# Up projection of a hybrid encoder: three row pairs by seven products in five groups of eleven, and the gate rows in two lots

## The chip, the cores and the metric

The kernel runs on one core of a Trainium2 chip. The metric is the device time of one execution in microseconds (us). Engines are named as the profile names them: PE is TensorE (matrix products), PEld its weight loads, DVE is VectorE, ACT is ScalarE, POOL is GpSimd and SP is SyncE, which only issues transfers here.

## The reference

Two layers of an encoder act on x, 256 positions by 2048 channels, in float32. Each layer has two halves:

```
h = RMSNorm(x)
[q | k | v | gu | gv] = h @ w_in
attn = windowed attention with QK norm, rotary and a sink   (1024 wide)
sgu  = gelu(gu) * (W_s @ LayerNorm(gelu(gv)) + b_s)           (1024 wide)
x = x + concat(RMSNorm(attn), RMSNorm(sgu)) @ w_o
[g | u] = DWConv3( RMSNorm(x) @ w_up )                         (2048 -> 2 x 5632)
x = x + (silu(g) * u) @ w_down                                 (5632 -> 2048)
```

The change touches the product with `w_up` and, in the mixing half, the gains of the gated rows ahead of `w_o`.

## The kernel before

**Precision.** A float32 product is made from float32r products of a high and a low part. For a weight block, ScalarE writes the high part (`his`, L192, L274, L281) and VectorE the low part (`los`, L166) as the raw block less the high part. Activations (`acts`) are kept as a high and a low tile. One product of one 128 x 128 activation block with one 128 x 512 weight block is three matmuls: low and high activation with the high weight, then high activation with the low weight.

**Up projection.** The 5632 hidden channels are cut into 11 groups of 512 (`j` = 0 to 10), and each group has two column blocks, n = 0 (gate, g) and n = 1 (up, u). The 2048 input channels are 16 row blocks (`k`). Positions are two blocks of 128 (`m`). A group is a list of blocks from `up_blocks(j)`. A plain block (`direct`, L231) takes four row blocks of one n: one load of 1024 KB, one ScalarE copy, one VectorE subtraction, and 4 x 2 x 3 = 24 matmuls, the 16 with the high weights first and the 8 with the low ones after. Groups 0 to 4 come first, then the first half of the down projection, then groups 5 to 10 and the second half of the down projection.

**Seven products.** Two row blocks, two positions blocks and two column blocks form a product of 2 x 2 by 2 x 2 block matrices, eight block products, or 24 matmuls. `seven` (L268) forms it from seven block products, in the manner of Strassen and Winograd: 21 matmuls. It needs sums of the four weight blocks, made on VectorE in a second raw tile (L278 for two of them at once, L279, L280), high parts of three raw blocks (L274) and of the four sums (L281), their low parts (L166, 1536 and 2048 wide), and sums of the activation blocks, made once (`mixed`, L259) and split (`parts`). Three of the seven products belong to extra sums in PSUM (`extra`: one double tile and two single ones, `tp`). After the last sevenfold block of a group, `added` (L318) turns them into the rows that `leave` adds to the plain sums. The first matmuls of a sevenfold block use L274's output, then three use the 1536-wide low part, then eight use L281's output and four the low part of the sums.

Groups j in `UP_FAST` = 1, 3, 6, 8 are made so (fast groups), with the row pairs in `UP_PAIRS`, that is rows 0, 1 and rows 2, 3. Their order is plain n=0, plain n=1, seven, plain n=0, seven, plain n=1, plain n=0, plain n=1: six plain blocks and two sevenfold ones. Other groups have eight plain blocks. The down projection has sevenfold blocks as well; they are not changed.

**Buffers.** Raw tiles (`rawp`): four of 1024 KB. Split weights: three wide places, used in turn; a sevenfold block takes two raw tiles and two places, a plain one takes one of each. PSUM: three double tiles and two single ones; a fast group uses them all. Everything else lives in 54 slots (`sl`).

**Between blocks.** When a column block's sum is finished, `leave` copies it out with the norm's scale (L958, or L961 and L962 with the extra rows) and spreads its words into 16-bit halves (L964). Transposing DMAs on SP (L972) turn them, ScalarE joins the halves again (`together`, L534), and the convolution follows on ScalarE (L943) and VectorE (L944, L947). For n = 0 that ends in SiLU (`gate_in`, L984); for n = 1 in the product (L992) and its split (L395, L396), and in some groups in sums for the down projection (`up_in`, L263 to L265, L402). These steps are put in a list, and `let_in` takes the next of them after the first products of a block. The order on each engine is planned ahead by priority and by readiness in the planner's own time; weights and these steps have a raised priority, in the order of the program. Every engine then runs its list in that order.

**Ahead of it.** Blocks of `w_o` go through `out_rows` (L908), first four column blocks c over the attention rows, then four over the gated rows. At c = 1 of the first four, all four pairs of gated rows are multiplied (`gate`, L880, with their squares) and then, at raised priority, gained and split into eight tiles (`gained`, L387 on ScalarE, L388 on VectorE). At c = 2 the sums of squares are asked for (`inv_rms_cols`: one addition, two PE transposes, one reduction, a power on POOL). `next_rows` prepares the rows of the up projection in the second four and makes the sums of activation blocks for the pairs in `UP_PAIRS`.

Of the kernel before, what the change touches and what calls it, by code (L numbers as in the profile page):

```python
# [28 lines left out]
KB = 4  # L29
# [6 lines left out]
HALVES = ((0, 20), (20, NF))  # L36
FAST = (((4, 8, 12), (4, 8, 12, 16)), ((4, 8, 12, 16), (4, 8, 12, 16)))
AFTER = (((2, 4, 5), (1, 2, 3, 4)), ((2, 4, 5, 6), (2, 4, 5, 6)))
UP_FAST = (1, 3, 6, 8)
UP_PAIRS = (0, 2)  # L40
UP_AFTER = (2, 3)
PLACES = 6


# [12 lines left out]
def up_blocks(j):  # L57

    if j not in UP_FAST:
        rows = [tuple(range(k, k + KB)) for k in range(0, NK, KB)]  # L60
        if j == 0:
            return [((n,), ks, False) for ks in rows for n in range(2)]
        return [((n,), ks, False) for n in range(2) for ks in rows]
    plain = [k for k in range(NK) if k - k % 2 not in UP_PAIRS]
    own = [((n,), tuple(plain[i : i + KB]), False) for i in range(0, len(plain), KB) for n in range(2)]
    for i, k in enumerate(UP_PAIRS):
        own.insert(UP_AFTER[i] + i, ((0, 1), (k, k + 1), True))
    return own


C_N1, C_AG, C_SG, C_N2, C_CW = 0, 16, 24, 32, 48
# [6 lines left out]
def encoder(ctx: ExitStack, tc: tile.TileContext, xT, x, w_in, w_gu, w_o, w_up, w_down, wsT, pcol, prow, rope, out):  # L78
# [12 lines left out]
    def sl(shape, dt=F32):  # L91
        return slots.tile(shape, dt, tag="sl", name="sl")
# [22 lines left out]
    def urgent():  # L115
        return tc.high_priority(offset=AHEAD)
# [8 lines left out]
    with urgent():  # L125
        pc = lay.tile([P, N_COL], F32, tag="pc", name="pc")
# [191 lines left out]
    def added(more):  # L318

        t, v, r, z = row(), row(), row(), row()  # L320
        with urgent():
            nc.scalar.copy(t, more[0])
            nc.vector.tensor_tensor(out=v, in0=t, in1=more[1], op=ALU.subtract)
            nc.vector.tensor_tensor(out=r, in0=more[2], in1=v, op=ALU.subtract)
            nc.vector.tensor_tensor(out=v, in0=v, in1=more[3], op=ALU.subtract)
            nc.vector.tensor_tensor(out=z, in0=r, in1=more[3], op=ALU.add)
        return [[t, v], [r, z]]
# [57 lines left out]
    def split_act(src, g):  # L385
        t = sl([P, 2, SEQ], F32R)
        nc.scalar.activation(t[:, 0, :], src, AF.Copy, scale=g)  # L387
        nc.vector.scalar_tensor_tensor(  # L388
            out=t[:, 1, :], in0=src, scalar=g, in1=t[:, 0, :].bitcast(F32), op0=ALU.mult, op1=ALU.subtract
        )  # L390
        return t
# [36 lines left out]
    def inv_rms_cols(acc, n, tag):  # L428
        nc.vector.tensor_tensor(out=acc[:, 0, :], in0=acc[:, 0, :], in1=acc[:, 1, :], op=ALU.add)
        got = st([P, 2], tag + "r")  # L430

        def turned():
            t = tp([P, 2, P])
            for m in range(2):
                nc.tensor.transpose(t[:, m, :], acc[:, 0, m * P : (m + 1) * P], ident)
            v = st([P, 2], tag + "s")
            nc.vector.tensor_reduce(out=v, in_=t, axis=AX.X, op=ALU.add)
            inv_rms(v, n, tag, 2, got)

        waiting.append(turned)  # L440
        return got
# [96 lines left out]
    def rotate(rows, m, nh, tab):  # L538
        v = rows.rearrange("p (h d) -> p h d", d=HD)
        a = sl([P, nh, HD])  # L540
        nc.vector.tensor_tensor(
            out=a, in0=v, in1=tab[:, 0, m, :].unsqueeze(1).to_broadcast([P, nh, HD]), op=ALU.mult
        )
        b = sl([P, nh, HD])
        for lo, hi in ((0, 64), (64, 0)):
            nc.vector.tensor_tensor(
                out=b[:, :, lo : lo + 64],
                in0=v[:, :, hi : hi + 64],
                in1=tab[:, 1, m, lo : lo + 64].unsqueeze(1).to_broadcast([P, nh, 64]),
                op=ALU.mult,  # L550
            )
        nc.vector.tensor_tensor(out=a, in0=a, in1=b, op=ALU.add)
        return a
# [7 lines left out]
    def gained(tiles, g0, pc):  # L561
        return [split_act(t[:, i, :], pc[:, g0 + 2 * j + i : g0 + 2 * j + i + 1]) for j, t in enumerate(tiles) for i in range(2)]
# [109 lines left out]
    def next_rows(c, gain, pcs, far=False):  # L672
# [14 lines left out]
        def joined_halves():  # L687
            for j in range(2):
# [4 lines left out]
                for i in range(2):  # L693
                    hT.append(split_act(t[:, i, :], col(i)))
                if gain == C_N2 and 2 * (2 * c + j) in UP_PAIRS:
                    y = sl([P, 2, SEQ])
# [33 lines left out]
    for l in range(DEPTH):  # L730
        pc, qk = params
# [47 lines left out]
        for m in range(2):  # L779
            a = rotate(kv[m][:, : 2 * HD], m, 2, tabs[1])  # L780
# [61 lines left out]
        sg, fs = [], []  # L842
# [37 lines left out]
        def gate(u):  # L880
            with urgent():
                nc.vector.tensor_tensor(out=sg[u], in0=sg[u], in1=fs[u], op=ALU.mult)
                add_squares(accs, sg[u], u == 0)
# [16 lines left out]
        gates = []  # L900
# [7 lines left out]
        def out_rows(half, c, r):  # L908
            t = mm()
            ps = [t[:, m, :] for m in range(2)]  # L910
            for b in range(2):
                src = w_o[l, c, :, (half * 2 + b) * KB * W : (half * 2 + b + 1) * KB * W]
                rows_by_cols(ps, (atts, gates)[half][b * KB : b * KB + KB], src, b == 0, b == 1)
            residual(ps, c, r)

        ra = inv_rms_cols(acca, D // 2, "a")
        for c in range(4):
            if c == 1:
                for u in range(4):
                    gate(u)  # L920
                with urgent():
                    gates.extend(gained(sg, C_SG, pc))
            if c == 2:
                rs = inv_rms_cols(accs, D // 2, "s")
            out_rows(0, c, ra)
        for c in range(4):
# [50 lines left out]
        def gate_and_up(j, ys, mixes):  # L977
# [9 lines left out]
            def up_in(tall):  # L987
                for i in range(2):
# [7 lines left out]
                    if k in FAST[half][0] + FAST[half][1]:  # L996
                        e = mixed(y)
                        waiting.append(lambda e=e, k=k: mixes.__setitem__(k, parts(e, [P, W])))

            blocks = up_blocks(j)  # L1000
            sums, fresh, more = {}, {}, [None, None]
            at = j * 2 * NK * W
            n_fast = 0
            for i, (ns, ks, sevenfold) in enumerate(blocks):
# [8 lines left out]
                if sevenfold:  # L1013
                    if n_fast == 0:
# [4 lines left out]
                        sums[0], sums[1], extra, acts, up_mixes[n_fast - 1], src,  # L1019
                        fresh[0], fresh[1], n_fast == 1, n_fast == len(UP_PAIRS),  # L1020
                    )
                    if n_fast == len(UP_PAIRS):
                        more = added(extra)
# [8 lines left out]
        for half, (f0, f1) in enumerate(HALVES):  # L1032
# [25 lines left out]
            for group in range(2):  # L1058
# [4 lines left out]
                for n, (cs, ks, sevenfold) in enumerate(blocks):  # L1063
# [26 lines left out]
                    c = cs[0]  # L1090
# [88 lines left out]
```

## Time and profile before

| | us |
|---|---|
| median of 3 runs | 1943.15 |
| lowest, highest | 1943.05, 1944.77 |
| profiled execution | 1943.45 |
| its span | 1941.6 |
| PE, DVE, ACT busy in the span | 1934.0, 1517.0, 1372.1 |

The span runs from the first to the last instruction of the program; the 1.85 us around it belong to the execution too. A row of the groups gives line, engine, operation, tiles and shapes, count, busy time, mean length of one in ns, and the idle time of the engine before it with what ended it. A row of the timeline gives the start in us from the span's start, the length, engine, line and operation, and in brackets the idle time before it. Matmuls overlap each other, so that their recorded length is longer than the step from one to the next. In layer 0 the up projection's groups 0 to 4 run from 269.56 to 485.52 us: group 1 starts at 313.10, group 2 at 356.32, group 3 at 399.84 and group 4 at 442.00.

### The profile page before, as it was taken

Reading aid. Unit: us, or ns where it says so; the run is one execution under the profiler, and the core shown is the slowest. Engines: PE = TensorE matmul, PEld = TensorE weight load, DVE = VectorE, ACT = ScalarE, POOL = GpSimd, SP = SyncE. Lnnn points to the kernel's source line nnn. Section 1 sums busy time; section 2 is a strip of 40 time slices with the busy share of each in tenths; the row PEclk is TensorE's granted clock in tenths of the full one; section 3 lists DMA queues with packets and bytes.
Section 4 is the critical chain, followed back from the end, with each engine's and each line's share of the span. In section 5 each row is a group of like instructions: output and inputs, shape, how many; then the busy total and the mean of one; then the engine's idle time right before and its main releaser. Section 6 shows DMA issues by size and latency. Waiting matters only on the chain.

```text
span 1941.6 us, 23236 instructions
## 1 busy us (share of the span) xinstructions
PE 1934.0 (100%) x8742; PEld 1604.8 (83%) x8742; DVE 1517.0 (78%) x1876; ACT 1372.1 (71%) x1509; POOL 22.9 (1%) x25
## 2 busy tenths in 40 slices
PE   9999999999999999999999999999999999999999
PEld 8888788888888888888888888888888888888887
DVE  5759776887886878689867796778869867886896
ACT  6776487887755787776676864888776557887753
POOL 0100000000000000000000000000000000000000
PEclk9999999999999999999999999999999999999999
DMA  9764586767556767656677446867675557577563
GB/s 361 221 201 152 183 248 176 260 216 211 186 220 214 231 192 259 203 193 227 228 217 249 146 154 216 239 193 228 233 224 182 222 203 238 183 242 228 178 240 130
DMA packets 191024, 414.04 MB, mean 213 GB/s; under 512 B 139456, under 2 KB 140736, under 8 KB 146112
## 3 DMA queue, kind: packets, MB, share of 16 engines
q1 hardware_dynamic: 190192, 411.83, 64.5%
q8 instruction: 68, 1.11, 0.2%
q10 hardware_dynamic: 720, 0.73, 0.1%
q14 instruction: 44, 0.36, 0.1%
HBM read 378.43 MB, written 2.10 MB: 196 GB/s over the span
## 4 chain that ended last, share of the span: by engine, by line
PE 96%; DVE 2%; ACT 1%; DMA 1%; issue 0%; SPq 0%; POOL 0%; DVEq 0%; ACTq 0%
PE mm L238 58%; PE mm L220 13%; PE mm L225 7%; PE mm L364 3%; PE mm L304 3%; PE mm L298 3%; PE mm L299 2%; PE mm L369 2%; PE tp L238 1%; PE tp L304 1%; PE tp L298 1%; PE tp L299 1%; DVE los L166 1%; DMA sl<-sl 1%; PE tp L407 0%; PE tp L637 0%
## 5 line engine op out<-in xcount | busy, mean ns | idle before, releaser
L166 DVE TENSOR_TENSOR los<-raw,his 128x2048 fp32r<-128x2048 f32 (+3 forms) x492 | 895.3, 1830 | 305.3 <-ACT his L192 152.7
L238 PE MATMUL mm<-his,sl 128*128 128x512 f32 x3424 | 811.6, 389 | 0.0
L238 PEld LDWEIGHTS mm<-his,sl 128*128 128x128 f32 x3424 | 642.8, 188 | 133.4
L192 ACT ACTIVATE his<-raw 128x2048 fp32r<-128x2048 f32 (+1 forms) x220 | 415.8, 1894 | 127.8 <-PE mm L238 92.7
L238 PE MATMUL mm<-los,sl 128*128 128x512 f32 x1712 | 423.1, 389 | 0.0
L238 PEld LDWEIGHTS mm<-los,sl 128*128 128x128 f32 x1712 | 321.4, 188 | 66.7
L220 PE MATMUL mm<-his,sl 128*128 128x512 f32 x1152 | 310.7, 391 | 0.4 <-ACT his L181 0.4
L181 ACT ACTIVATE his<-raw 128x1024 fp32r<-128x1024 f32 (+1 forms) x180 | 185.9, 1038 | 143.9 <-PE mm L220 118.7
L220 PEld LDWEIGHTS mm<-his,sl 128*128 128x128 f32 x1152 | 215.4, 188 | 45.2 <-ACT his L181 0.8
L225 PE MATMUL mm<-los,sl 128*128 128x512 f32 x576 | 178.1, 390 | 1.3 <-DVE los L166 1.3
L534 ACT COPY sl<-sl 128x1024 uint16<-128x1024 uint16 x98 | 132.4, 1351 | 56.2 <-DMA sl<-sl 55.7
L281 ACT ACTIVATE his<-raw 128x2048 fp32r<-128x2048 f32 x46 | 88.0, 1913 | 64.3 <-DVE raw L280 38.6
L225 PEld LDWEIGHTS mm<-los,sl 128*128 128x128 f32 x576 | 108.0, 188 | 23.9 <-DVE los L166 1.7
L943 ACT ACTIVATE sl<-sl,pc 128x256 f32<-128x256 f32 x176 | 95.5, 590 | 1.3
L964 ACT COPY sl<-sl 128x1024 uint16<-128x1024 uint16 x88 | 90.4, 1041 | 1.5
L298 PE MATMUL mm<-his,sl 128*128 128x512 f32 x234 | 91.3, 390 | 0.0
L299 PE MATMUL mm<-his,sl 128*128 128x512 f32 x234 | 91.0, 389 | 0.0
L274 ACT ACTIVATE his<-raw 128x1536 fp32r<-128x1536 f32 x46 | 68.3, 1484 | 28.6 <-PE mm L238 19.1
L944 DVE SCALAR_TENSOR_TENSOR sl<-sl,pc 128x255 f32<-128x255 f32 x176 | 79.2, 479 | 8.3 <-ACT sl L943 7.5
L395 ACT ACTIVATE sl<-sl 128x256 fp32r<-128x256 f32 x88 | 31.8, 409 | 71.0 <-DVE sl L992 71.0
L947 DVE SCALAR_TENSOR_TENSOR sl<-sl,pc 128x255 f32<-128x255 f32 x176 | 78.1, 478 | 0.6
L304 PE MATMUL mm<-los,sl 128*128 128x512 f32 x234 | 75.7, 390 | 0.9 <-DVE los L166 0.9
(156 smaller groups left out, 1520.8 us busy)
## 6 DMA issues: line engine op xcount, KB each, us to landing
raw<-in_w_up SPq DMA_DIRECT2D x176, 1024.0 KB, 4.7
raw<-in_w_down SPq DMA_DIRECT2D x86, 1024.0 KB, 4.6
raw<-in_w_in SPq DMA_DIRECT2D x38, 1024.0 KB, 5.2
raw<-in_w_o SPq DMA_DIRECT2D x32, 1024.0 KB, 4.9
raw<-in_w_gu SPq DMA_DIRECT2D x16, 1024.0 KB, 5.3
sl<-sl SPq DMA_TRANSPOSE x244, 3.7
sl<-in_prow SPq DMA_DIRECT2D x12, 256.0 KB, 7.4
raw<-in_w_in SPq DMA_DIRECT2D x8, 256.0 KB, 5.3
```

Source lines behind the costliest of these rows:

```text
L166: nc.vector.tensor_tensor(out=lo, in0=part, in1=hi.bitcast(F32), op=ALU.subtract)
L181: nc.scalar.activation(hi[:, cs], part, AF.Copy)
L192: nc.scalar.activation(hi[:, :n], raw[:, :n], AF.Copy)
L220: nc.tensor.matmul(ps[m], acts[kk][:, part, m * P : (m + 1) * P], hi, start=first and kk == 0 and part == 0, stop=False,)
L225: nc.tensor.matmul(ps[m], acts[kk][:, 0, m * P : (m + 1) * P], lo, start=False, stop=last and kk == KB - 1)
L238: nc.tensor.matmul(ps[m], acts[kk][:, part % 2, m * P : (m + 1) * P], w, start=first, stop=done and kk == len(acts) - 1 and part == 2,)
L298: nc.tensor.matmul(ps[m], a[0], w[0][:, cs], start=new, stop=False)
L299: nc.tensor.matmul(ps[m], a[1], w[0][:, cs], start=False, stop=False)
L304: nc.tensor.matmul(ps[m], a[0], w[1][:, cs], start=False, stop=ps is more and last)
L534: nc.scalar.copy(words, tall.rearrange("p (b a) n -> p b (a n)", b=2))
L943: nc.scalar.activation(t[:, i, :], s[:, i, :], AF.Identity, bias=col(3), scale=col(1))
L964: nc.scalar.copy(h, rows.bitcast(U16).rearrange("p (j n b) -> p j b n", j=2, b=2))
```

## The change

The fast groups become j = 1, 3, 5, 7, 9, and each has three sevenfold pairs, with rows 0 to 5. Ten plain row blocks are left. They are now cut into 2 + 4 + 4, the short cut first, so that a fast group is half n=0, half n=1, seven, plain n=0, seven, plain n=1, seven, plain n=0, plain n=1: nine blocks where there were eight. A half block loads 512 KB and has 12 matmuls. The weights are laid out on the host by the same list of blocks. `next_rows` makes one more set of sums of activation blocks, for rows 4 and 5.

The gated rows are multiplied, gained and split in two lots, pairs 0 and 1 at c = 1 and pairs 2 and 3 at c = 2, and the sums of squares are asked for at c = 3.

```diff
-UP_FAST = (1, 3, 6, 8)
-UP_PAIRS = (0, 2)
-UP_AFTER = (2, 3)
+UP_FAST = (1, 3, 5, 7, 9)
+UP_PAIRS = (0, 2, 4)
+UP_AFTER = (2, 3, 4)
@@ up_blocks
     plain = [k for k in range(NK) if k - k % 2 not in UP_PAIRS]
-    own = [((n,), tuple(plain[i : i + KB]), False) for i in range(0, len(plain), KB) for n in range(2)]
+    cuts = [0, *range(len(plain) % KB or KB, len(plain) + 1, KB)]
+    own = [((n,), tuple(plain[a:b]), False) for a, b in zip(cuts, cuts[1:]) for n in range(2)]
     for i, k in enumerate(UP_PAIRS):
         own.insert(UP_AFTER[i] + i, ((0, 1), (k, k + 1), True))
@@ w_o, first four column blocks
         for c in range(4):
-            if c == 1:
-                for u in range(4):
+            if c in (1, 2):
+                us = (2 * c - 2, 2 * c - 1)
+                for u in us:
                     gate(u)
                 with urgent():
-                    gates.extend(gained(sg, C_SG, pc))
-            if c == 2:
+                    for u in us:
+                        gates.extend(gained([sg[u]], C_SG + 2 * u, pc))
+            if c == 3:
                 rs = inv_rms_cols(accs, D // 2, "s")
             out_rows(0, c, ra)
```

## The prediction

> **What bounds the kernel now.** I read the page first, then the waits of TensorE alone, then the chain that ended last, then windows over the up-projection groups of the first layer.
>
> ```profile
> span 1941.6 us, 23236 instructions
> ...
> PE 1934.0 (100%) x8742; PEld 1604.8 (83%) x8742; DVE 1517.0 (78%) x1876; ACT 1372.1 (71%) x1509; POOL 22.9 (1%) x25
> ```
>
> TensorE has work in the whole span. Its recorded waits, of this view the two rows that the change can touch:
>
> ```profile
> PE mm L225 <- DVE los L166: 1.3, 1, 1.3
> ...
> PE mm L304 <- DVE los L166: 0.9, 2, 0.7
> ```
>
> So TensorE nearly never waits, and a matmul saved is worth one step of its pace. The chain of waits gives the pace, from long unbroken runs:
>
> ```profile
> 340.15 70.73 PE mm L238 x312
> ...
> 659.42 70.72 PE mm L238 x312
> ```
>
> 70.73 / 312 = 0.2267 us from one 512-wide matmul to the next. (The 389 ns that the groups show for one is its own length, overlapping the next.) A block of 24 takes 5.44 us, a sevenfold block of 21 takes 4.76 us, a half block of 12 takes 2.72 us.
>
> The windows of groups j=1, 2 and 3 of layer 0 (TensorE, its loads, VectorE, ScalarE, GpSimd, clock, DMA share, GB/s) show who could become the bound:
>
> ```profile
> 313.10:356.32 43.22, 42.55 (x188) 34.76 (x186) 33.79 (x40) 32.78 (x34) 0.00 (x0) 1.00 0.78 238
> 356.32:399.84 43.52, 43.52 (x194) 36.04 (x192) 36.39 (x45) 41.69 (x47) 0.00 (x0) 1.00 0.68 205
> 399.84:442.00 42.16, 42.16 (x188) 34.91 (x186) 36.78 (x42) 32.36 (x32) 0.00 (x0) 1.00 0.68 240
> ```
>
> j=1 and j=3 are sevenfold already, with two pairs. VectorE is the next engine: 36.78 of 42.16 us in j=3. The clock is full throughout.
>
> **The products.** A sevenfold block does 21 matmuls where its two row blocks and two column groups took 24: 3 x 0.2267 = 0.68 us. Before, 4 groups x 2 pairs x 2 layers = 16 such blocks; after, 5 x 3 x 2 = 30. The other 14 save 42 matmuls: 42 x 0.2267 = **9.52 us**. The Trainium skill (TensorE: Matmul & The Clock Gate, "Wait — 56ns, not 53.3ns?") has 215.7 ns between warm 512-wide matmuls; by that these would be 9.06 us. The trace's 226.7 ns decides.
>
> **What they cost on VectorE and ScalarE.** These are the groups by shape that a block issues:
>
> ```profile
> L166 DVE TENSOR_TENSOR los<-raw,his 128x2048 fp32r<-128x2048 f32 x262 | 597.4, 2287 | 201.3 <-ACT his L192 152.7 <-ACT his L281 47.5 <-PE tp L299 0.4
> ...
> L166 DVE TENSOR_TENSOR los<-raw,his 128x1024 fp32r<-128x1024 f32 x176 | 212.3, 1220 | 79.3 <-ACT his L181 69.6 <-PE mm L369 8.5 <-PE mm L225 0.6
> ...
> L281 ACT ACTIVATE his<-raw 128x2048 fp32r<-128x2048 f32 x46 | 88.0, 1913 | 64.3 <-DVE raw L280 38.6 <-PE mm L238 22.5 <-PE mm L299 3.1
> ...
> L166 DVE TENSOR_TENSOR los<-raw,his 128x1536 fp32r<-128x1536 f32 x46 | 80.6, 1752 | 22.9 <-PE mm L238 15.2 <-ACT his L274 7.7
> ...
> L274 ACT ACTIVATE his<-raw 128x1536 fp32r<-128x1536 f32 x46 | 68.3, 1484 | 28.6 <-PE mm L238 19.1 <-PE mm L299 7.8 <-ACT his L192 1.6
> ...
> L278 DVE TENSOR_TENSOR raw<-raw 128x1024 f32<-128x1024 f32 x46 | 56.2, 1221 | 25.9 <-DMA raw<-in_w_up 25.3 <-DMA raw<-in_w_down 0.3
> ...
> L280 DVE TENSOR_TENSOR raw<-raw 128x512 f32<-128x512 f32 x46 | 31.7, 688 | 0.9
> ...
> L192 ACT ACTIVATE his<-raw 128x1024 fp32r<-128x1024 f32 x4 | 4.2, 1053 | 3.7 <-DVE los L166 3.7
> ```
>
> A sevenfold block asks VectorE for 1.22 + 2 x 0.69 + 1.75 + 2.29 = 6.64 us, a plain one for 2.29, a half one for 1.22. A fast group trades two plain blocks for one sevenfold and two halves: 6.64 + 2.44 - 4.58 = +4.50 us on VectorE. On ScalarE: 1.48 + 1.91 + 2 x 1.05 - 2 x 1.91 = +1.67 us. For j=3 that makes VectorE 36.78 + 4.50 = 41.3 of 42.16 - 0.68 = 41.5 us; ScalarE 34.0. VectorE would be full in a fast group. In a whole layer it stays covered, because the fast groups now alternate with slow ones; the question is the lateness inside one group.
>
> **Lateness in j=3 (7 and 9 alike).** The lookahead is three wide places and four raw tiles; one sevenfold block takes two of each. The order becomes half, half, S1, plain, S2, plain, S3, plain, plain, so S1 starts 5.44 us after the group instead of 10.88. In the timeline of before, S1's last low part (407.64), S2's (419.59) and where TensorE uses that (424.77):
>
> ```profile
> 407.64 2.29 DVE L166 TENSOR_TENSOR los<-raw,his 128x2048 fp32r<-128x2048 f32 x1
> ...
> 419.59 2.29 DVE L166 TENSOR_TENSOR los<-raw,his 128x2048 fp32r<-128x2048 f32 x1
> ...
> 421.79 0.87 DVE L944 SCALAR_TENSOR_TENSOR sl<-sl,pc 128x255 f32<-128x255 f32 x2
> ...
> 424.77 0.39 PE L304 MATMUL mm<-los,sl 128*128 128x512 f32 x1
> ```
>
> S2's parts were 424.77 - 421.88 = 2.9 us early. VectorE's next instruction starts 0.08 us before the last one's recorded end (419.59 + 2.29 = 421.88 against 421.79), so I count each 0.08 less. S1's part, ready at 409.93 here, is wanted at 399.84 + 5.44 + 17 x 0.2267 = 409.13; its two halves free their places earlier, so I cost S1 at nothing (0.8 at most). From 409.93 VectorE has to do: a plain low part 2.21, S2's low parts 3.88, a plain 2.21, S3's sums and first low part 2.36 + 1.67, and the convolution step of the group before (`up_in`), of these groups:
>
> ```profile
> L944 DVE SCALAR_TENSOR_TENSOR sl<-sl,pc 128x255 f32<-128x255 f32 x176 | 79.2, 479 | 8.3 <-ACT sl L943 7.5
> ...
> L992 DVE TENSOR_TENSOR sl<-sl 128x512 f32<-128x512 f32 x44 | 30.3, 689 | 0.8
> ...
> L396 DVE TENSOR_TENSOR sl<-sl 128x256 fp32r<-128x256 f32 x88 | 33.2, 418 | 2.9 <-ACT sl L395 2.9
> ...
> L402 DVE TENSOR_TENSOR sl<-sl 128x512 fp32r<-128x512 f32 x30 | 20.6, 687 | 10.1 <-ACT sl L401 10.1
> ...
> L263 DVE TENSOR_TENSOR sl<-sl 128x256 f32<-128x256 f32 x20 | 8.3, 417 | 0.0
> ...
> L264 DVE TENSOR_TENSOR sl<-sl 128x128 f32<-128x128 f32 x20 | 5.7, 285 | 0.1
> ```
>
> 8 x 0.40 + 2 x 0.61 + 4 x 0.34 + 0.61 + 0.34 + 2 x 0.20 = 7.1 us. Together 19.5 us: 429.4. S3 starts at 399.84 + 2 x 2.72 + 2 x 4.76 + 2 x 5.44 = 425.68 and wants that part 6 matmuls on, at 427.04: **2.3 us late** if VectorE never idles and the whole step stands ahead. That is the upper end. The lower end is 0: `up_in` may be ordered behind S3, and TensorE can do the next plain block's 16 high products (3.6 us) meanwhile, which need ScalarE only. The nearest row is the sevenfold block of the down projection at 522.24, which also follows a sevenfold and one plain block with an `up_in` between; there four plain products stand inside it:
>
> ```profile
> 522.24 0.39 PE L298 MATMUL mm<-his,sl 128*128 128x512 f32 x1
> ...
> 526.40 1.07 PE L238 MATMUL mm<-his,sl 128*128 128x512 f32 x4
> ...
> 528.23 1.99 PE L238 MATMUL mm<-his,sl 128*128 128x512 f32 x8
> ```
>
> 528.23 - 522.24 = 5.99 us for 25 matmuls that take 5.67: 0.3 lost. I take 0.3 for each of j=3, 7, 9 in two layers: **+1.8 us** (0 to 13.8). j=5 follows the down projection and has no `up_in`: 0.
>
> **Lateness in j=1.** There both steps of j=0 fall in, and before already waits:
>
> ```profile
> 319.98 1.36 ACT L534 COPY sl<-sl 128x1024 uint16<-128x1024 uint16 x1 [3.23 <-DMA sl<-sl]
> 321.20 1.91 ACT L281 ACTIVATE his<-raw 128x2048 fp32r<-128x2048 f32 x1
> ...
> 321.44 0.69 DVE L280 TENSOR_TENSOR raw<-raw 128x512 f32<-128x512 f32 x1
> ...
> 323.14 2.29 DVE L166 TENSOR_TENSOR los<-raw,his 128x2048 fp32r<-128x2048 f32 x1 [1.01 <-ACT his L281]
> ...
> 338.96 0.50 PE L304 MATMUL mm<-los,sl 128*128 128x512 f32 x1 [0.67 <-DVE los L166]
> ```
>
> ScalarE sits on L534 for a transposed tile still on its way, with S1's high part of the sums (L281) queued behind it, VectorE's low part behind that, and TensorE behind both. S1 will be wanted 5.44 us sooner. But its place is also free sooner (a half block holds it), so L281 can stand ahead of L534. I let the waits of this group double: **+0.9 us** (-0.9 if they vanish; +5.5 by the second rival).
>
> **The gates.** In layer 0 VectorE works through eight gains before the low part that TensorE waits for:
>
> ```profile
> 199.76 2.06 DVE L388 SCALAR_TENSOR_TENSOR sl<-sl,pc 128x256 fp32r<-128x256 f32 x5
> 201.74 3.49 DVE L166 TENSOR_TENSOR los<-raw,his 128x1024 fp32r<-128x1024 f32 x3
> ```
>
> This is the 1.3 us row above. Two lots put four gains (4 x 0.41) and their products behind it, more than the wait: **-1.3 us** (0 if the second lot makes such a wait itself). The moved square sum, its two transposes, its reduction and GpSimd's power come one column block later, still two blocks ahead of their first use: 0. The third mix per layer is two ScalarE copies and five small VectorE operations in the second half of w_o, where TensorE had no wait: 0, or their 1.7 us per layer uncovered.
>
> **Loads.** The bytes are the same. In each of the 10 fast groups two half loads stand where one whole one would, one instruction more on SP for the transposes to queue behind.
>
> ```profile
> raw<-in_w_up SPq DMA_DIRECT2D x176, 1024.0 KB, 4.7
> ...
> raw<-in_w_down SPq DMA_DIRECT2D x4, 512.0 KB, 3.3
> ```
>
> A half load lands in 3.3 us against 4.7, so a pair takes 2 x 3.3 - 4.7 = 1.9 us more, at a DMA share of 0.7 beside matmuls: 0. The Trainium skill (DMA: Bandwidth & Descriptors, "Bandwidth") asks for DMAs of 1 MiB or more; the rows agree that a half load carries less per us, and the ten pairs would add 19 us if nothing covered them.
>
> **Sum.** 1943.45 (the profiled execution; its span and 1.85 us around it) - 9.52 + 1.8 + 0.9 - 1.3 = 1935.3. The median of the runs is 0.3 lower: **1935.0 us**.
>
> **Rivals.** *All hidden:* no new wait, j=1's gone: 1943.15 - 9.5 - 1.3 - 0.9 = 1931.4. For: slack of 2.9 us at S2, TensorE's room to reorder. Against: VectorE at 41.3 of 41.5 us.
> *Transposes eat it:* L281 stays behind L534 in j=1. It ends at 323.1, wanted at 318.54 + 9 x 0.2267 = 320.6; the low part ends at 325.4, wanted at 322.4: 3.0 us in each layer, and the step behind it as late: with 1 us more for S3, 8 instead of 0.9: 1942. For: that order stands in the trace. Against: the place frees earlier.
> *VectorE becomes the bound, slower:* every `up_in` stands whole ahead of S3: 2.3 us in six groups, 13.8 instead of 1.8, and in j=1, from S2's sums at 322.1, the same list with both steps (2.2 + 3.9 + 2.2 + 4.0 + 3.2 + 5.8 = 21.3) ends at 343.4 against 313.10 + 25.84 + 1.36 = 340.3: 3.1 us per layer, 6.2 instead of 0.9. Together 1952.3. It decides once the fast groups lose over 5.4 us a layer more than now. For: the budget. Against: in j=3 the slack falls only from 399.84 + 10.88 + 3.85 - 409.93 = 4.6 us at S1 to 2.9 at S2, with `up_in` between.
>
> **Chances.** Forecast 0.42, all hidden 0.16, transposes 0.22, VectorE 0.20. What a measurement can tell from no change is 0.2%, 3.9 us: faster 0.58, same 0.22, slower 0.20. The range runs from just under all hidden to the near part of the VectorE rival: 1930.3 to 1950; the forecast's own is 1932.5 to 1938.5.
>
> **What would show it.** TensorE's instructions fall by 42 and its 0.2267 us stays. Right: waits on los at L304 grow to about 3 us in all, the 1.3 us at L225 is gone, VectorE is nearly full in the windows of j=3, 7, 9. Wrong: waits on los above 10 us, or at L298 on ScalarE's his behind L534; fresh waits at L225 or on the square-sum transposes.

## The result: 0.7% slower, and the profile after

| | before | after |
|---|---|---|
| median, us | 1943.96 (4 runs) | 1956.73 (4 runs) |
| lowest, highest, us | 1943.05, 1944.79 | 1955.41, 1957.99 |
| profiled execution, its span, us | 1943.45, 1941.6 | 1955.41, 1953.6 |

The ratio is 1.0067, with a 95% interval of 1.0052 to 1.0081. The forecast was 1935.0 us; the change costs 12.8 us instead of saving 8. Lines of the changed kernel stand one later than before up to about L920 and three later behind that (L958 of before is L961 here).

The page of the changed kernel, head and chain of waits:

```profile
span 1953.6 us, 23380 instructions
...
PE 1932.8 (99%) x8700; PEld 1597.1 (82%) x8700; DVE 1584.7 (81%) x1966; ACT 1397.6 (72%) x1541; POOL 21.3 (1%) x25
...
PE 84%; ACT 5%; DVE 5%; DMA 2%; issue 2%; SPq 0%; DVEq 0%; ACTq 0%
```

TensorE has its 42 matmuls fewer (8700 for 8742), but the chain that ended last, TensorE's nearly alone before, now runs through ScalarE, VectorE and transfers for 12% of the span. The waits of TensorE say where (line that waits, what it waits for, us in total, times, longest):

```profile
PE mm L299 <- ACT sl L961: 4.3, 2, 2.2
PE mm L239 <- ACT sl L388: 3.7, 2, 2.2
PE mm L239 <- DVE sl L389: 3.2, 2, 1.6
PE mm L305 <- DVE los L167: 2.9, 5, 1.0
...
PE tp L299 <- ACT his L282: 0.9, 2, 0.5
```

The wait for gates (L225 before) is gone. Two places are new and large, each once in both layers: group 0's plain products wait for split activations (L388, L389), and the first sevenfold block of group 3 waits for a PSUM tile that ScalarE has still to copy out (L961).

**The start of the up projection.** The queue of SP around the last columns of `w_o` in layer 0, before (start, length, line, operation, count):

```profile
269.93 8.09 SPq L190 DMA_DIRECT2D raw<-in_w_up  x3
278.07 5.15 SPq L684 DMA_TRANSPOSE sl<-sl  x4
283.88 0.33 SPq L190 DMA_DIRECT2D raw<-in_w_up  x1
```

and after:

```profile
268.71 13.52 SPq L191 DMA_DIRECT2D raw<-in_w_up  x4
282.32 6.07 SPq L685 DMA_TRANSPOSE sl<-sl  x4
```

Before, the third column's transposes (L684) stood behind three loads of up weights; after, behind four. A load can't go until VectorE has finished with a raw tile, and what stands behind it on SP waits too. SP's waits between 262 and 292 us after (what waits, for what, us in total, times, longest):

```profile
SPq L191 <- DVE los L167: 16.0, 4, 5.0
```

The transposes start at 282.32 instead of 278.07, 4.25 us later, though SP came to the first of these loads 1.22 us sooner. The timeline after shows what that does (in brackets the idle time before, and what ended it):

```profile
288.18 1.35 ACT L692 COPY sl<-sl 128x1024 uint16<-128x1024 uint16 x1 [4.03 <-DMA sl<-sl]
...
291.33 2.29 DVE L167 TENSOR_TENSOR los<-raw,his 128x2048 fp32r<-128x2048 f32 x1 [6.44 <-ACT his L193]
291.75 0.73 PE L239 MATMUL mm<-his,sl 128*128 128x512 f32 x2 [1.46 <-ACT sl L388]
...
294.07 2.32 PE L239 MATMUL mm<-his,sl 128*128 128x512 f32 x9 [1.59 <-DVE sl L389]
```

ScalarE sits idle for 4.03 us on the joining of that column (L692); VectorE idles 6.44 us behind ScalarE; TensorE waits twice. In layer 1 the same waits have a tail:

```profile
1262.30 0.73 PE L239 MATMUL mm<-his,sl 128*128 128x512 f32 x2 [2.22 <-ACT sl L388]
1264.63 7.09 PE L239 MATMUL mm<-his,sl 128*128 128x512 f32 x23 [1.59 <-DVE sl L389]
1271.55 1.98 PE L239 MATMUL mm<-los,sl 128*128 128x512 f32 x8
```

From 1264.63 to 1271.55 are 6.92 us for 23 matmuls that take 23 x 0.2267 = 5.21: 1.7 us more. The windows over them and behind them give the reason in the third last column, the granted clock (0.76, then 1.00):

```profile
1264.60:1271.60 7.00, 6.97 (x24) 5.61 (x25) 3.45 (x4) 3.51 (x5) 0.00 (x0) 0.76 0.82 170
1271.60:1276.00 4.40, 4.40 (x21) 3.66 (x20) 1.96 (x1) 4.40 (x5) 0.00 (x0) 1.00 0.50 207
```

**Group 3.** It starts at 402.67, before at 399.84. SP ahead of it, before:

```profile
387.93 5.47 SPq L972 DMA_TRANSPOSE sl<-sl  x4
394.26 0.33 SPq L190 DMA_DIRECT2D raw<-in_w_up  x1
```

ScalarE, SP and TensorE at its front, after:

```profile
394.03 0.33 SPq L191 DMA_DIRECT2D raw<-in_w_up  x1
394.46 5.19 SPq L975 DMA_TRANSPOSE sl<-sl  x4
...
400.22 1.35 ACT L535 COPY sl<-sl 128x1024 uint16<-128x1024 uint16 x1 [3.81 <-DMA sl<-sl]
...
407.27 1.91 ACT L282 ACTIVATE his<-raw 128x2048 fp32r<-128x2048 f32 x1
...
409.59 1.91 ACT L193 ACTIVATE his<-raw 128x2048 fp32r<-128x2048 f32 x1
...
412.32 0.69 ACT L961 ACTIVATE sl<-mm,yr 128x512 f32<-128x512 f32 x1
...
413.07 0.50 PE L299 MATMUL mm<-his,sl 128*128 128x512 f32 x1 [2.08 <-ACT sl L961]
```

Again a load (394.03) stands ahead of transposes (L975), which stood ahead of it before. ScalarE idles 3.81 us for them, and all that it does next is late: the second copy of group 2's PSUM tile (L961), which stands behind S1's high part (L282) in its list, ends at 413.01. The extra sums of group 3 need that tile; S1 starts at 408.11, two half blocks behind the group's start. Before, S1 came 10.88 us behind it, at 410.72, and the second copy (L958) was done at 404.71:

```profile
404.02 0.69 ACT L958 ACTIVATE sl<-mm,yr 128x512 f32<-128x512 f32 x1
```

In layer 1 the window at the same place shows the granted clock down to 0.83 behind a wait of 2.19 us:

```profile
1382.00:1392.00 10.00, 7.81 (x28) 6.07 (x27) 9.26 (x7) 9.06 (x9) 0.00 (x0) 0.83 0.72 191
```

### The profile page after: what moved, and what is told of

It reads as the page before. It is cut to its first block, busy times and chain, and to the rows that moved or that the text cites. A ratio compares the mean times of both kernels' runs of the same rounds, so it can differ in the third digit from the quotient of the medians.

```text
span 1953.6 us, 23380 instructions
## 1 busy us (share of the span) xinstructions
PE 1932.8 (99%) x8700; PEld 1597.1 (82%) x8700; DVE 1584.7 (81%) x1966; ACT 1397.6 (72%) x1541; POOL 21.3 (1%) x25
## 4 chain that ended last, share of the span: by engine, by line
PE 84%; ACT 5%; DVE 5%; DMA 2%; issue 2%; SPq 0%; DVEq 0%; ACTq 0%
PE mm L239 45%; PE mm L221 13%; PE mm L226 7%; PE mm L305 3%; DVE los L167 3%; PE mm L299 3%; PE mm L300 3%; PE mm L365 3%; DMA sl<-sl 2%; PE mm L370 2%; ACT sl L535 1%; PE tp L305 1%; PE tp L299 1%; PE tp L239 1%; PE tp L300 1%
## 5 line engine op out<-in xcount | busy, mean ns | idle before, releaser
L167 DVE TENSOR_TENSOR los<-raw,his 128x2048 fp32r<-128x2048 f32 (+3 forms) x516 | 920.9, 1797 | 265.3 <-ACT his L193 95.1
L239 PEld LDWEIGHTS mm<-his,sl 128*128 128x128 f32 x3200 | 601.3, 188 | 134.2 <-ACT sl L388 4.5
L193 ACT ACTIVATE his<-raw 128x2048 fp32r<-128x2048 f32 (+1 forms) x216 | 390.3, 1816 | 114.7 <-PE mm L239 75.8
L239 PEld LDWEIGHTS mm<-los,sl 128*128 128x128 f32 x1600 | 300.3, 188 | 62.4
L221 PEld LDWEIGHTS mm<-his,sl 128*128 128x128 f32 x1152 | 214.9, 188 | 45.8 <-ACT his L182 1.1
L282 ACT ACTIVATE his<-raw 128x2048 fp32r<-128x2048 f32 x60 | 114.8, 1913 | 113.2 <-DVE raw L281 80.9
L535 ACT COPY sl<-sl 128x1024 uint16<-128x1024 uint16 x98 | 132.3, 1350 | 17.5 <-DMA sl<-sl 17.5
L226 PEld LDWEIGHTS mm<-los,sl 128*128 128x128 f32 x576 | 108.0, 188 | 22.5
L275 ACT ACTIVATE his<-raw 128x1536 fp32r<-128x1536 f32 x60 | 89.1, 1484 | 35.6 <-PE mm L239 25.4
L305 PE MATMUL mm<-los,sl 128*128 128x512 f32 x304 | 100.3, 394 | 2.9 <-DVE los L167 2.9
L279 DVE TENSOR_TENSOR raw<-raw 128x1024 f32<-128x1024 f32 x60 | 73.3, 1222 | 7.5 <-DMA raw<-in_w_up 6.7
```

The lines of the kernel that those rows point to most:

```text
L167: nc.vector.tensor_tensor(out=lo, in0=part, in1=hi.bitcast(F32), op=ALU.subtract)
L193: nc.scalar.activation(hi[:, :n], raw[:, :n], AF.Copy)
L221: nc.tensor.matmul(ps[m], acts[kk][:, part, m * P : (m + 1) * P], hi, start=first and kk == 0 and part == 0, stop=False,)
L226: nc.tensor.matmul(ps[m], acts[kk][:, 0, m * P : (m + 1) * P], lo, start=False, stop=last and kk == KB - 1)
L239: nc.tensor.matmul(ps[m], acts[kk][:, part % 2, m * P : (m + 1) * P], w, start=first, stop=done and kk == len(acts) - 1 and part == 2,)
L282: nc.scalar.activation(shi, sums, AF.Copy)
```

## The experiments

Each has the medians of its runs beside the kernel before on the same chip (1943.3 to 1943.9 us). Runs of one kernel lie up to 7.8 us apart. The intervals of the ratios reach some 0.1% (2 us) to either side, up to 0.17% (3.3 us) where a kernel had four or five runs, so less than 2 us between two medians isn't read as a difference.

**The parts.** The gates alone: the kernel before with the second hunk of the diff. 

> The kernel before with the two lots of gates alone. Late-transposes theory and vector theory agree: the wait of 1.3 us of TensorE on the low part in the first w_o columns of layer 0 goes, nothing else changes: 1.4 us less than before, about 1942.5 us; no wait on los at the first w_o columns.

Measured: 1941.66, ratio 0.9988 (0.9978 to 0.9998). The wait at L225 is gone, and the other one that the change could touch is still there (L304, 1.3 us in two waits, 0.9 before). The gates gain 2.1 us, and nothing of the loss is theirs.

Five groups, two pairs:

```diff
-UP_PAIRS = (0, 2, 4)
-UP_AFTER = (2, 3, 4)
+UP_PAIRS = (0, 2)
+UP_AFTER = (2, 3)
```

> The changed kernel with two row pairs in the five groups instead of three (whole blocks, no half ones, and no third set of sums of activations). It has 20 sevenfold blocks for 16 of before, 12 matmuls less: 2.7 us. Late-transposes theory: without the third set the transposes of the third w_o column stand again ahead of the load, and S1 comes again two whole blocks after the start of its group, so the waits at the start of the up projection (9.8 us) and at group 3 (6.4 us) are gone: 1943.9 - 2.7 - 1.4 = 1940 us, TensorE waiting under 3 us in all. Vector theory: five fast groups still load VectorE more than four did, about 1 us of waits on los in each of groups 7 and 9: 1943 to 1945 us.

Measured: 1944.4, ratio 1.0003 (0.9994 to 1.0012). Against the gates alone it has one fast group more, 12 matmuls or 2.7 us less of TensorE, and is 2.7 us slower. The waits on L388 and L389 and on the PSUM copy aren't there; 3.9 us on a high part (L193) are, at other places. So the third pair brings the loss of 12 us, but a fifth group pays nothing either.

Three pairs, but in four groups:

```diff
-UP_FAST = (1, 3, 5, 7, 9)
+UP_FAST = (1, 3, 6, 8)
```

> The changed kernel with its three pairs in the four groups 1, 3, 6, 8 of before. 24 sevenfold blocks, 24 matmuls less than before: 5.4 us. Late-transposes theory: the waits at the start of the up projection (9.8 us over before) and at group 3 (6.4 us) stay whole, the one in group 5 goes: 1943.9 - 5.4 - 1.4 + 9.8 + 6.4 + 3.5 = 1957 us, as slow as the change. Vector theory: the loss is shared out over the fast groups with a convolution step in them, so with one group less it falls by a fifth, and nothing is lost ahead of group 1: about 1952 us.

Measured: 1965.03, ratio 1.0107 (1.0092 to 1.0122), slower still and above both theories, with the same waits as after (4.1 us on L961, 3.2 on L389, 3.1 on L388) and 2.8 more on L193. The loss doesn't come from the number of fast groups.

**The third set of sums.** The changed kernel, its third set of sums of activations made four blocks later, in group 0:

```diff
+                    if 2 * (2 * c + j) < 4:
+                        mix()
+                    else:
+                        after(MIX_WAIT, mix)
```

> The changed kernel, with the third set of sums of activations made four blocks later, in group 0 of the up projection, instead of ahead of it. The work is the same. Late-transposes theory: the transposes of the third w_o column stand ahead of the load of group 1's first half block again, TensorE's waits on the split activations at the start of the up projection (9.8 us over both layers, slow steps of TensorE after them included) go, the 6.4 us at group 3 stay: about 1947 us. Vector theory: VectorE has the same work, in group 0 rather than ahead of it: no change within 1 us, 1956 us.

Measured: 1944.89, ratio 1.0005 (0.9995 to 1.0014): 11.8 us of the loss are gone, with the waits on L388 and L389. What is left:

```profile
PE mm L300 <- ACT sl L970: 3.8, 2, 1.9
PE mm L306 <- DVE los L168: 3.4, 7, 0.9
```

On SP the third column's transposes stand behind three loads again. But the set's own work has moved too; which of the two it is, the runs on SP's order below tell.

**Moving what is left.** The PSUM copy raised above all else, and the half blocks put last, both on top of the later set:

```diff
-                with urgent():
+                with first_of_all() if more is None else urgent():
```
```diff
+    cuts = [0, 4, 8, 10]
```

> The kernel with the late third set, and in it the copy out of PSUM of a finished column block at the highest priority, so that ScalarE does it two instructions (about 2.4 us) sooner at the start of group 3. PSUM theory: S1 of group 3 waits for the PSUM tile of group 2's last column block, as its half blocks bring it 5.4 us after the group's start; with the copy sooner the waits on that copy (2.0 + 2.1 us) go: 1944.9 - 4.1 = about 1941 us. Vector theory: what is lost in the fast groups is VectorE's time, and the wait only moves to S1's or S3's low part: 1944 to 1945 us.

> The kernel with the late third set, and the cut of its ten plain row blocks into 4 + 4 + 2 instead of 2 + 4 + 4: the half blocks end a fast group, S1 starts 10.9 us after the group's start as in the kernel before. PSUM theory: the waits on the copy out of PSUM at group 3 (4.1 us) go, and the later S1 leaves VectorE 5.4 us more ahead of S3, so most of the 3.4 us on los at S3 go as well: about 1939 us, if the shorter tail (5.4 us instead of 10.9 after S3) makes no new wait for the extra sums. Vector theory: VectorE's work per group is the same, and it is full: waits only move into the next group: 1943 to 1945 us.

Measured: 1944.17, ratio 1.0005 (0.9996 to 1.0015), and 1956.51, ratio 1.0061 (1.0044 to 1.0078). In the first the waits on los grow to 5.3 us while those on the PSUM copy shrink to 3.2: the wait moves. In the second they are 8.3 us, with others on VectorE of 3.4 and 2.3, and the time is 11.6 us above that with the half blocks first; neither theory had that. Having them first is not what costs; where the new waits come from stays open.

**VectorE lighter.** The third tap of the convolution left out, in the changed kernel with the later set (first), in before with the gates (second, the control) and in the changed kernel itself (third).

> The kernel with the late third set, without the third tap of the convolution (the line that adds the next position's value is left out, 176 VectorE instructions of 0.48 us, 84 us of VectorE). Vector theory: TensorE's waits on los (3.4 us) and on the sums' high part come from VectorE's load, so they fall under 1 us; the wait on the copy out of PSUM stays at about 4 us: 1941 us. Order theory: these waits come from what stands ahead in the queues (loads, transposes, ScalarE), not from VectorE's load, and stay: 1944 to 1945 us.

> Control for the run without the third tap: the kernel before with the two lots of gates, and the third tap of the convolution left out (176 VectorE instructions, 84 us). Vector theory: with two pairs in four groups VectorE keeps up anyway, so only the 1.3 us of waits on los at group 1's second sevenfold block can go: 1941.7 - 1.5 = about 1940 us, and the changed kernel without the tap (1936.2) is then faster by about 4 us, as its fewer matmuls promise less its wait of 3.4 us at group 1. If the tap costs time by itself, in a chain that ends last: 1935 us or below.

> The changed kernel as it is, the third set of sums ahead of the up projection, without the third tap of the convolution. Two-causes theory: the 11.8 us at the start of the up projection come from the transposes that stand behind a load on SP, where no convolution runs yet, so they stay, and VectorE's 8.7 us go: 1956.7 - 8.7 = about 1948 us, with TensorE's waits on the split activations near 7 us. If both are VectorE's load: about 1936 us.

Measured: 1936.18, ratio 0.9963 (0.9948 to 0.9978); 1942.01, ratio 0.9992 (0.9983 to 1.0002); 1946.77, ratio 1.0015 (1.0005 to 1.0024). The tap is worth nothing where VectorE has room (1942.01 for 1941.66; 1940 was expected), 8.7 us with the later set, 10.0 in the changed kernel. The first run is faster than either of its theories, and the wait on the PSUM copy, which both left standing, went too; 3.1 us on the sums' high part (L283) stand in group 1. In the third run the waits on L388 and L389 stay (3.7 and 3.2), those on los and the PSUM copy are gone, and the 3.1 us on the high part in group 1 are there as well: the loss at the start stays with a lighter VectorE. But the lighter VectorE has also changed the planned order on SP (group 2's transposes stand ahead of the load there), so these runs don't part fullness from order.

**Work moved to GpSimd**, with the later set: two of the four weight sums, and the product of gate and up.

```diff
-            nc.vector.tensor_tensor(out=s[:, 2, :], in0=s[:, 0, :], in1=b[:, 2, :], op=ALU.add)
-            nc.vector.tensor_tensor(out=s[:, 3, :], in0=s[:, 2, :], in1=b[:, 1, :], op=ALU.add)
+            nc.gpsimd.tensor_tensor(out=s[:, 2, :], in0=s[:, 0, :], in1=b[:, 2, :], op=ALU.add)
+            nc.gpsimd.tensor_tensor(out=s[:, 3, :], in0=s[:, 2, :], in1=b[:, 1, :], op=ALU.add)
```
```diff
-                    nc.vector.tensor_tensor(out=y, in0=y, in1=t, op=ALU.mult)
+                    nc.gpsimd.tensor_tensor(out=y, in0=y, in1=t, op=ALU.mult)
```

> The kernel with the late third set, and the last two of the four sums of weight blocks of every sevenfold block on GpSimd instead of VectorE (120 additions of 128x512, 0.69 us each on VectorE: 83 us off VectorE, 4.1 us per fast group). GpSimd's time for them stands in no trace here. Vector theory: if GpSimd needs no more than about 2 us for one, the fast groups lose their waits on los: 1937 to 1940 us. If it is slower, or slows VectorE beside it, the sums' high part comes late and waits on ScalarE's his take the place: 1945 us or more.

> The kernel with the late third set, and the product of gate and up (44 of 128x512, 0.69 us each on VectorE, 30 us) on GpSimd. It stands in no chain that a sevenfold block waits for. Vector theory: a third of the relief of the left out tap, spread in the same places: 1944.9 - 3 = about 1942 us. If GpSimd slows VectorE beside it by as much as it takes off: 1945 us.

Measured: 1979.61, ratio 1.0185 (1.017 to 1.02), and 2019.07, ratio 1.0386 (1.037 to 1.0401). The groups of the first, by shape:

```profile
L282 POOL TENSOR_TENSOR raw<-raw 128x512 f32<-128x512 f32 x60 | 140.1, 2335 | 4.7
...
L168 DVE TENSOR_TENSOR los<-raw,his 128x1536 fp32r<-128x1536 f32 x60 | 122.6, 2043 | 28.7 <-PE mm L240 17.8 <-ACT his L276 10.7
```

GpSimd needs 2335 ns for what VectorE does in 686, and VectorE's own low part beside it takes 2043 ns instead of 1752. The sums come later than before: TensorE waits 7.2 us for their high part (L283), and 8.4 us for the rows that `added` makes (L325). In the second kernel the product takes 2760 ns, and TensorE waits 26.9 us for the sums' high part. Neither theory had that: the product was thought to stand in no chain that a sevenfold block waits for. How it gets into one stays open.

**The order on SP.** Now the changed kernel's work as it is, with a rule for SP's order: a load recorded so many loads behind four transposes may not be planned ahead of them.

```diff
+    def load(dst, src):
+        loads[0] += 1
+        ins = next((i for n, i in reversed(behind) if loads[0] >= n), None)
+        if ins is None:
+            nc.sync.dma_start(dst, src)
+        else:
+            with tc.issue_after(ins):
+                nc.sync.dma_start(dst, src)
+    def ahead_of_load(n):
+        behind.append((loads[0] + n, latest(mybir.EngineType.SP)))
@@ next_rows, behind its transposes
+            if gain == C_N2:
+                ahead_of_load(10)
@@ leave, behind its transposes
+                ahead_of_load(7)
```

The first run has only the call in `next_rows`, the second only the one in `leave`, the third both; the fourth is the control, before with the gates and both.

> The changed kernel with its work unchanged; only the tenth load recorded behind the four transposes of a column of w_o may not stand ahead of them on SP. In the plan the transposes of the third column of w_o then stand ahead of the first half load of group 1 instead of behind it. If SP's order is the cause of the late start of the up projection: the waits on L388 and L389 of the changed kernel (3.7 and 3.2 us) go and the time falls from 1956.7 to about 1945, as with the third set of sums made later. If the third set's own work on ScalarE and VectorE at that place is the cause: those waits stay and the time stays at 1955 to 1958.

> The changed kernel with its work unchanged; only the seventh load recorded behind the four transposes of an up group's sums may not stand ahead of them on SP. If a load that stands ahead of these transposes is what makes ScalarE late at group 3 (it sits idle for 3.8 us at 396.4 for a transposed tile, and the copy of the PSUM tile comes behind that): the wait of 4.3 us on the PSUM copy at L299 goes, with the 1.8 us of slow steps behind it in layer 1; 1956.7 becomes about 1950.5, and less if the waits on los go too. If VectorE's fullness alone sets it: the wait only moves, 1955 to 1958.

> Both orders in the changed kernel. If SP's order is behind both losses: 1938 to 1939, some 5 us under the kernel before. If only the start of the up projection goes: 1945.

> Control: the kernel before with the two lots of gates and with both orders of the loads. It has hardly a wait left that they could take away (1.3 us on los at L304): 1941 to 1942, within 1 us of the same kernel without them. If it falls by more, the orders help for another reason than the change.

Measured: 1945.59, ratio 1.0011 (1.0001 to 1.002); 1954.54, ratio 1.0058 (1.0043 to 1.0073); 1942.34, ratio 0.9995 (0.9985 to 1.0004); control 1941.94, ratio 0.9988 (0.9979 to 0.9997). SP in the first, at the place shown in the result:

```profile
268.05 8.28 SPq L169 DMA_DIRECT2D raw<-in_w_up  x3
276.43 5.20 SPq L699 DMA_TRANSPOSE sl<-sl  x4
281.71 7.67 SPq L169 DMA_DIRECT2D raw<-in_w_up  x2
```

With three loads ahead of the transposes 11.1 us are gone, and with them the waits on activations at the start. Nothing else changed: in the two traces TensorE, VectorE, ScalarE and GpSimd run the same instructions in the same order, and on SP one load in each layer stands in another place. The third set's own work costs nothing that can be seen; its place in SP's order does.

In the groups the rule is worth 2.2 us alone, less than four runs of each can tell, and 3.3 on top of the first, and not the 6 that its theory expected: the PSUM wait goes altogether, but the waits on los grow. SP and ScalarE ahead of group 3 with this rule alone:

```profile
394.15 5.48 SPq L989 DMA_TRANSPOSE sl<-sl  x4
...
398.32 1.36 ACT L549 COPY sl<-sl 128x1024 uint16<-128x1024 uint16 x1 [1.05 <-DMA sl<-sl]
...
407.39 0.69 ACT L975 ACTIVATE sl<-mm,yr 128x512 f32<-128x512 f32 x1
407.98 1.91 ACT L296 ACTIVATE his<-raw 128x2048 fp32r<-128x2048 f32 x1
```

The transposes go out only 0.3 us sooner than in the changed kernel (394.46). But there the load issued at 394.03 was still under way, and they took 2.7 to 5.2 us to land; here they take 2.4 to 2.5, and ScalarE goes on 1.9 us sooner (398.32 for 400.22). So in group 3 it was the load's transfer, and not its wait for a buffer, that made the transposes late. The planner has also put the second PSUM copy (L975 here) ahead of S1's high part (L296), and moved some steps of VectorE and products of S1, so that these runs don't tell what SP's order is worth by itself in the groups.

In the kernel with both rules, whose profiled execution was the slowest of its ten (1945.50):

```profile
PE mm L319 <- DVE los L181: 7.3, 6, 1.6
```

and there VectorE, ahead of S3's first low part in group 3 (L293 to L295 are the sums of the weight block; L963 and L966 are the convolution, L1012 the product behind it and L279 one of the sums of `up_in`):

```profile
423.66 1.22 DVE L293 TENSOR_TENSOR raw<-raw 128x1024 f32<-128x1024 f32 x1
424.80 0.28 DVE L279 TENSOR_TENSOR sl<-sl 128x128 f32<-128x128 f32 x1
425.00 0.48 DVE L963 SCALAR_TENSOR_TENSOR sl<-sl,pc 128x255 f32<-128x255 f32 x1
...
427.38 0.69 DVE L295 TENSOR_TENSOR raw<-raw 128x512 f32<-128x512 f32 x1
427.98 0.68 DVE L1012 TENSOR_TENSOR sl<-sl 128x512 f32<-128x512 f32 x1
428.58 3.95 DVE L181 TENSOR_TENSOR los<-raw,his 128x1536 fp32r<-128x1536 f32 x2
...
430.39 0.97 PE L319 MATMUL mm<-los,sl 128*128 128x512 f32 x3 [1.65 <-DVE los L181]
```

VectorE goes without a gap from 417.89 on, most of the step between blocks woven in ahead of the low part, and TensorE waits 1.65 us.

**What is left then.** Both orders without the third tap, and the later set with the order in the groups:

> The changed kernel with both orders, without the third tap of the convolution (left out: 176 VectorE operations, 84 us; the output is that of a two-tap convolution). On SP it stands as in the kernel with both orders but for one load in two groups of each layer. If the waits on los that remain there (7.3 us at L319) are VectorE's fullness: they go, 1942.3 becomes 1933 to 1935, while the same cut gave the two lots of gates alone nothing (1941.7 to 1942.0). If they come from the order of the loads that still differs: 1939 or above.

> The third set of sums made later, and the transposes of an up group's sums ahead of the seventh load behind them. Against the third set made later alone (1944.9): if the order in the groups is worth the 2.2 to 3.3 us that it gave in the two runs before, 1942; if the later set has already taken that, 1945. Under 1941.6 it would beat every version so far.

Measured: 1937.39, ratio 0.9964 (0.9951 to 0.9977), and 1943.42, ratio 0.9999 (0.9989 to 1.0009). The lighter VectorE, with the order on all engines planned anew, gains 5.0 us, less than the 7 to 9 expected: group 3's waits on los are gone, but 3.1 us on a high part and 2.3 on los stay, nearly all in group 1. The second lies between its two theories, 1.5 us under the later set alone and not to be told from it. The fastest kernel of all that compute the reference stays before with the two lots of gates, 1941.66; with both orders set, the three pairs come to 1942.34, level with it.

## Why the prediction was wrong

The account by medians, in us: 1943.96, less 2.1 for the gates, less 9.5 for 42 matmuls, makes 1932.4. The order on SP at the start adds 11.1 (1956.73 less 1945.59), the order in the groups 3.3 (1945.59 less 1942.34), VectorE's load 5.0 (1942.34 less 1937.39). The remaining 5.0 (1937.39 less 1932.4) have 5.4 us of waits in the last trace beside them, but no run tells those apart. Only the 11.1 us have a single cause shown, by one moved load in each layer; for the 3.3 and the 5.0 the planned orders of ScalarE and VectorE changed as well.

- **The products: right.** 42 matmuls fewer, and where nothing waits the step is 0.2267 us as before.
- **The gates: right**, 2.1 us measured for 1.3; the difference is below what the runs tell apart.
- **"The third mix per layer is two ScalarE copies and five small VectorE operations in the second half of w_o, where TensorE had no wait: 0": this step failed.** Its own work was priced, at 1.7 us a layer if uncovered, and that was not the cost. Adding it moved the transposes of one column behind one more load in SP's planned order, and that load waits for VectorE to finish with a raw tile. The transposes were the last thing that the up projection's first products needed. Measured: 11.1 us in two layers by the medians, 9.45 between the two profiled executions (1955.41 and 1945.96); of these 3.7 and 3.2 are recorded waits and 1.7 slow steps.
- **"A DMA share of 0.7 beside matmuls: 0" for the loads, "one instruction more on SP for the transposes to queue behind": this named the right queue and priced the wrong thing.** At the start of the up projection a load cost SP its wait for a raw tile, 5.0 us at the longest; in group 3 its transfer made the transposes behind it land up to 5.2 us after their issue instead of 2.4. The share of 0.7 is a mean: from 394.4 to 399.7 it was 0.92. Setting the order in the groups gained 3.3 us, ScalarE's changed order included.
- **"I cost S1 at nothing (0.8 at most)": failed.** It was reckoned from VectorE's parts alone. S1 two half blocks earlier also needs the extra PSUM tile 5.44 us earlier, and ScalarE's copy of it came behind. In group 3 that was 4.3 us of recorded waits in the two layers.
- **Lateness in j=3, 7, 9, 1.8 us: right in size where it was looked for, by luck.** The waits on los in these groups sum to 1.7 us of the 2.9 at L305. But TensorE came to S3 2.1 us late already, after the PSUM wait; with that cured, the same block waits 1.65 us in group 3, near the 2.3 of the upper end. j=5, at 0, lost 0.5 us in each layer on L282.
- **Lateness in j=1:** 1.2 us of waits on los for 1.8 expected; L282 did not stay behind L535.
- **The rivals.** "VectorE becomes the bound" had the nearest time (1952.3) and a true mechanism, but its price of 17 us more was not what decided: the lighter VectorE gained 5 us where both orders were set, and 10 in the changed kernel. "Transposes eat it" named late transposes as the cause, at another place. None had the mechanism that cost most: a load, waiting for its buffer, ahead of transposes in one queue. (The prediction's "+5.5 by the second rival" for j=1 fits neither rival's own working, 3.0 us in each layer for the second and 3.1 for the third.)

None of the signs that were to show the forecast wrong appeared: the waits on los were below 10 us, those of L298's products on the high part short (0.9 us, in group 5), and there was none at L225. All that were to show it right did: 2.9 us on los, none at L225's place, and VectorE busy for 42.36 of the 44.48 us of j=3. The loss came where no sign had been set.

What stays open is why the plan puts the load ahead: it follows the planner's own reckoning of when each is ready.

## What to carry to other kernels

Read a queue by what its head waits for, and by what is still under way ahead of a small transfer: a load that waits for a buffer holds up every small transfer behind it, a load in flight can make it land later, and the engine that needs it holds up the rest. When a step is added, compare the planned order of the transfer queues before and after, since its own work may be the smallest part of its price. A block that moves earlier wants every resource earlier, its accumulator too, not only its operands.

## What the runs showed of the hardware

**Whether TensorE's clock fell hung on how much of a slot of 3.41 us it stood idle, not on the length of one wait.** In layer 1 of the changed kernel, waits of 2.22 and 1.59 us with two matmuls between them, and a single wait of 2.19 us in group 3, were followed by steps of 0.43 us instead of 0.227. The granted clock is 0.50 there, from 1264.82 and from 1384.28, for 3.41 us each, and these two starts are 119.46 us or 35 times 3.413 apart. Single waits of 1.91 us (three pairs in four groups, layer 1) and 1.93 us (the order at the start alone, layer 1) were followed by such a stretch too, while 2.08 us (group 3 of the changed kernel, layer 0) and 2.43 us (the product on GpSimd, ending at 441.74) left the clock at 1.00. All the traces agree once each is cut into slots of 3.413 us, counted from one of its falls: from 41 us on, a slot at full clock with 1.90 us or more of recorded idle time was followed by a fall, and none with 1.82 or less was. The 2.19 us had 1.96 in one slot; the 2.08 us were cut into 0.50 and 1.58. The ends of matmuls are modelled, so the bound is an estimate. The Trainium skill (TensorE: Matmul & The Clock Gate, "Part 1: The HAM clock gate (the "warmup" mystery)") has the clock at half after an idle window of some 3.4 us that runs freely. The doubled step, the length and the free running agree with the traces; that a whole window must stand idle does not, since 1.90 of 3.41 us were enough, and here the measurement decides.

**Transposes land later while a load is under way.** In the trace of the changed kernel, 175 transposes that SP issued while a load of its own had not landed took 4.4 us to land in the median, the other 69 took 2.5.

**GpSimd is no relief for VectorE here.** A 128x512 float32 sum took 2335 ns there and 686 on VectorE, and a product 2760 (in the second of the two kernels); VectorE's 1536-wide subtraction beside the sums took 2043 ns for 1752. The Trainium skill (GPSIMD Engine Reference, "3.1 Elementwise — side-by-side cycle accounting") has a two-input float32 sum of 2048 elements 1.96 times as long on GpSimd as on VectorE; the rows here, with 512 elements, have 3.4 times.
